# The assumed durations of a list scheduler, set to those of a trace: one core, two layers of a hybrid trunk

## The chip, the cores and the metric

The kernel runs on one core of a Trainium2 chip (trn2). The metric is the device time of one execution in microseconds (us). A core has engines that run beside each other, each in the order in which its own instructions were written: TensorE (PE, with its weight loads as PEld), VectorE (DVE), ScalarE (ACT), GpSimd (POOL), and SyncE (SP), which issues DMAs here. An instruction that needs a result of another engine waits on a semaphore, and everything behind it on its own engine waits with it.

## The reference

Two layers, each `x <- x + W_out(mixer(RMSNorm(x)) * silu(gate))`, on 2048 rows of width 1024 in float32. Layer 0 is stick-breaking attention with 16 heads of 64:

```python
z = jnp.einsum('bthd,bshd->bhts', q[:, t0:kl], k[:, :kl]).astype(jnp.float32) * scale
mask = s_idx < t_idx
log_fail = jnp.where(mask, jax.nn.log_sigmoid(-z), 0.0)
later = lax.cumsum(log_fail, axis=3, reverse=True) - log_fail
a = jnp.where(mask, jnp.exp(jax.nn.log_sigmoid(z) + later), 0.0)
outs.append(jnp.einsum('bhts,bshd->bthd', a.astype(v.dtype), v[:, :kl]))
```

Layer 1 is multi-head latent attention (MLA) with 8 heads: queries and keys come from low-rank latents, are normed per head, a part of 64 is rotated, and a causal softmax follows. Both project into and out of width 1024 with products that the kernel splits into a high and a low part for precision.

## The kernel before

No order of instructions is written by hand. The program first records all work as operations (`Op`: an engine, an assumed duration in ns, the calls, what it depends on, a priority), and then `Sched.issue` plays them through once: for each engine it keeps the time at which the engine would be free, takes from those that are ready the operation that could start first (all that could start within 60 ns of the engine's being free count as equal, and then the lower priority number, that is the earlier work, goes first), issues it, and adds its duration. A result is taken to be usable on another engine a fixed `LAT` after that (120 ns for PE and ACT, 180 for DVE, 150 for POOL). Tiles in SBUF and PSUM come from rings of a few buffers, and a ring with no free buffer holds an operation back as well. What comes out is one order for each engine; the chip then runs it, with real waits. The durations stand in the helpers of the class `Chip`: `mm` (products on PE), `turn` (transpositions on PE), `tt` and `split_sb` (element-wise products and differences), `ts` (a tile times a scalar), `select` (the causal mask on POOL), `fill` (memset).

The work around the change:

- Layer 0 (lines of `proj0` and `attn0`) goes over 8 pairs of heads (`hp`) and 4 groups (`j`) of 512 rows. `proj0` makes q, k, v and gate of a stage with products `pj<-xn,w`, 24 of 512 columns for each of the four. `attn0` takes the 512 rows in four parts (`rt`) against the groups `g` of keys up to `j`. One unit is: two products `z<-ks,qd` into a PSUM bank (ring of 3), two sigmoids on ACT (`a<-z`, `z<-z`), a running product on DVE (`pp<-z,...`, a scan), the product `a<-a,pp` on POOL (and the mask `select` where `g` is `j`), four transpositions `t<-ident,a` on PE, a split of their result on ACT and DVE (`at<-t`), and, when four units are done, products `av<-at,vv`. The projection of the next stage is recorded behind each stage and given priorities spread over it, so that its products fill PE between the units.
- Then come the output projection of layer 0, the latents and gates of layer 1, and MLA (`proj1`, `attn1`): 8 heads by 4 groups, five products for a `z`, a maximum on DVE (`nm`), an exponential on ACT (`s<-z,nm`), a scaling on POOL (`s<-s,c,ri`), transpositions `t<-ident,s`, a split (`pt`), products `av<-pt,vv`. The output projection of layer 1 ends the program.

Of the kernel before, what the change touches and what calls it, by code (L numbers as in the profile page):

```python
# [11 lines left out]
F32 = mybir.dt.float32  # L12
# [3 lines left out]
ALU = mybir.AluOpType  # L16
# [261 lines left out]
def R(x):  # L278
    if isinstance(x, Buf):
        return x.tile  # L280
    return x.resolve() if isinstance(x, Ref) else x


def refs(*xs):
    return [x.all() if isinstance(x, Buf) else x for x in xs if isinstance(x, (Buf, Ref))]


class Chip:
# [4 lines left out]
        self.eng = {"dve": nc.vector, "pool": nc.gpsimd}  # L293

    def mm(self, out, l, r, start, stop, n=G):
        self.s.add("pe", max(n / 2.4, 107.0) + 3.0,
                   lambda: self.nc.tensor.matmul(R(out), lhsT=R(l), rhs=R(r), start=start, stop=stop),  # L297
                   refs(out), refs(l, r))

    def turn(self, out, src, ident):  # L300
        self.s.add("pe", 109.0, lambda: self.nc.tensor.transpose(R(out), R(src), R(ident)), refs(out), refs(src, ident))  # L301

    def act(self, out, src, func, n=G, bias=None, scale=None, accum=None):
        def call():
# [10 lines left out]
        self.s.add("act", 60.0 + 0.833 * n + 93.0 * extra, call, refs(out, accum), refs(src, bias, scale))  # L315

    def tt(self, eng, out, a, b, op, n=G):
        ns = 70.0 + 1.045 * n if eng == "dve" else 155.0 + 2.1 * n
        self.s.add(eng, ns, lambda: self.eng[eng].tensor_tensor(out=R(out), in0=R(a), in1=R(b), op=op),  # L319
                   refs(out), refs(a, b))  # L320

# [3 lines left out]
                   refs(out), refs(a, b))  # L325

    def ts(self, eng, out, a, s1, s2, op0=ALU.mult, op1=ALU.mult, n=G):
        ns = 60.0 + 0.6 * n if eng == "dve" else 90.0 + 1.3 * n
        self.s.add(eng, ns, lambda: self.eng[eng].tensor_scalar(out=R(out), in0=R(a), scalar1=R(s1), scalar2=R(s2),  # L329
                                                                op0=op0, op1=op1),  # L330
                   refs(out), refs(a, s1, s2))
# [33 lines left out]

    def select(self, x, base, fill):

        self.s.add("pool", 300.0,
                   lambda: self.nc.gpsimd.affine_select(out=R(x), in_=R(x), compare_op=ALU.is_ge, fill=fill, base=base,
                                                        pattern=[[-1, P]], channel_multiplier=1),  # L370
                   refs(x), refs(x))

    def fill(self, out, v):
        self.s.add("pool", 40.0, lambda: self.nc.gpsimd.memset(R(out), v), refs(out), [])

    def dma(self, out, src, kb):
        self.s.add("sp", kb * 1024 / 360.0 + 100.0, lambda: self.nc.sync.dma_start(out=R(out), in_=R(src)),
# [7 lines left out]
def trunk(ctx: ExitStack, tc: tile.TileContext, x, w0, wo0, g0, g1, wlat, wgate, gqa, gkva,  # L385
# [7 lines left out]
    C = Chip(nc, sched)  # L393
# [27 lines left out]
    ident = const.tile([P, P], F32, "ident")  # L421
    sched.add("pool", 1000.0, lambda: make_identity(nc, R(ident)), refs(ident), [])
    def causal(dst, base, fill):

        mtmp = pa.tile([P, G], F32, "tmp", 2)[:, 0:P]
        C.fill(mtmp, 0.0)
        C.select(mtmp, base, fill)
        C.copy("dve", dst, mtmp, P)
# [14 lines left out]

    def split_sb(hi, lo, src, n, eng="pool"):
        C.act(hi, src, AF.Copy, n)
        C.tt(eng, lo, src, hi.bitcast(F32), ALU.subtract, n)

    def rstd(pl, ss, n, dim, name, bufs=2):
        v = pl.tile([P, n], F32, name + "v", 2)
# [54 lines left out]
    def load_w(hp, u, early=None):  # L504
        w = pw.tile([P, 2, KD, P], F32R, "w", 4)
        for n, raw in enumerate(early or ()):
            k = slice(4 * n, 4 * n + 4)
            split_sb(w[:, 0, k], w[:, 1, k], raw, 4 * P, "dve" if n else "pool")
        if early:
            ws[hp, u] = w  # L510
            return
        for k in range(0, KD, 2):
            raw = pw.tile([P, 2, P], F32, "wraw", 4)
            C.dma(raw, w0[hp, u, :, k:k + 2, :], 128)
            split_sb(w[:, 0, k:k + 2], w[:, 1, k:k + 2], raw, 2 * P)
        ws[hp, u] = w
# [77 lines left out]
    def attn0(hp, j):  # L594
# [47 lines left out]
        yh = pa.tile([P, 2, G], F32R, "yh")  # L642
        C.tt("dve", y, y, gt, ALU.mult)
        split_sb(yh[:, 0, :], yh[:, 1, :], y, G)
        C.dma(y_d[j, :, hp], yh.all().bitcast(F32), 512)

# [514 lines left out]
```

## Time and profile before

| what | value |
|---|---|
| median of 3 runs | 3061.82 us (3061.26 to 3068.74) |
| the profiled execution | 3061.58 us, its span 3059.9 us |
| busy PE | 2978.5 us, 97% of the span, 15728 matmuls |
| busy DVE, ACT, POOL | 66%, 61%, 49% |
| mean granted TensorE clock | 0.996 |

The span runs from the first to the last instruction; 1.7 us of the execution lie around it. The profile's page gives each engine's busy time, then the span in 40 slices, the DMA queues, the chain of work that ended last, and groups of instructions with the idle time before them. A matmul's record is longer than the time after which the next one starts, since they are pipelined, so that a busy PE can still lose a little.

### The profile page before, as it was taken

How to read it: one execution, taken by the hardware profiler on the slowest of the kernel's cores; microseconds unless marked ns; L12 is line 12 of the kernel's file. 1: busy time of each engine (PE TensorE's matmuls, PEld its weight loads, DVE VectorE, ACT ScalarE, POOL GpSimd, SP SyncE). 2: the span in 40 equal slices, each digit the busy share in tenths (PEclk: the TensorE clock that was granted, in tenths of full speed). 3: DMA queues.
4: the chain of work that ended last, by engine and by line, in shares of the span. 5: the costliest groups of instructions: out<-in, count | busy, mean ns of one | idle time of the engine just before them, and what ended most of it. 6: DMA issues, size and time to landing. Idle time of an engine off the chain costs nothing.

```text
span 3059.9 us, 48542 instructions
## 1 busy us (share of the span) xinstructions
PE 2978.5 (97%) x15728; PEld 2486.1 (81%) x15728; DVE 2024.9 (66%) x3553; ACT 1865.3 (61%) x4635; POOL 1491.4 (49%) x2931
## 2 busy tenths in 40 slices
PE   8899999999999999999999999999999999999999
PEld 6678888888888888888778888878888888888787
DVE  5777896978868778787863231047778777778511
ACT  5676786867768677786852132247777776777400
POOL 4664664756647565574652120136456455555200
PEclk9899999999999999999999999999999999999999
DMA  6253334344243342433339673142222232223462
GB/s 241 104 172 124 130 105 140 109 138 148 81 152 103 125 152 83 150 112 115 126 122 324 243 274 117 69 158 83 78 92 72 86 104 66 75 78 93 160 219 103
DMA packets 134797, 399.87 MB, mean 131 GB/s; under 512 B 16656, under 2 KB 39696, under 8 KB 131984
## 3 DMA queue, kind: packets, MB, share of 16 engines
q1 hardware_dynamic: 134544, 396.76, 38.3%
q8 instruction: 126, 2.06, 0.3%
q14 instruction: 127, 1.04, 0.1%
HBM read 272.97 MB, written 98.57 MB: 121 GB/s over the span
## 4 chain that ended last, share of the span: by engine, by line
PE 75%; DVE 11%; ACT 7%; issue 3%; POOL 2%; DMA 2%; POOLq 0%; DVEq 0%; ACTq 0%; SPq 0%
PE pj L297 30%; PE z L297 21%; PE av L297 12%; PE t L301 9%; DVE pp L342 3%; PE t L297 3%; DVE at L319 1%; DVE pt L319 1%; PE pj L301 1%; ACT s L312 1%; ACT a L312 1%; DVE qs L329 1%; DVE y L319 1%; DVE nm L349 1%; ACT j L312 1%
## 5 line engine op out<-in xcount | busy, mean ns | idle before, releaser
L297 PE MATMUL pj<-xn,w 128*128 128x512 f32 x3072 | 863.6, 402 | 2.0 <-DVE qd L319 1.9
L319 POOL TENSOR_TENSOR a<-a,pp 128x512 f32<-128x512 f32 (+3 forms) x640 | 611.6, 958 | 474.0 <-DVE pp L342 437.4
L297 PEld LDWEIGHTS pj<-xn,w 128*128 128x128 f32 x3072 | 545.4, 188 | 100.0 <-issue 3.7
L342 DVE TENSOR_TENSOR_SCAN pp<-z,cy,a 128x512 f32<-128x512 f32 x384 | 484.1, 1273 | 43.8 <-ACT z L312 39.8
L312 ACT ACTIVATE at<-t 128x512 fp32r<-128x512 f32 (+3 forms) x640 | 340.8, 535 | 156.7 <-PE t L301 154.6
L319 DVE TENSOR_TENSOR at<-t,at 128x512 fp32r<-128x512 f32 (+3 forms) x640 | 377.8, 599 | 84.4 <-ACT at L312 79.5
L312 ACT ACTIVATE a<-z 128x512 f32<-128x512 f32 (+3 forms) x640 | 335.5, 535 | 115.7 <-PE z L297 93.0
L297 PE MATMUL z<-ks,qd 128*128 128x512 f32 (+3 forms) x1280 | 365.2, 377 | 13.7 <-DVE pp L342 9.0
L297 PE MATMUL av<-at,vv 128*128 128x512 f32 (+3 forms) x1280 | 376.1, 379 | 2.1 <-DVE at L319 2.1
L301 PE MATMUL t<-ident,a 128*128 128x128 f32 x2176 | 343.6, 274 | 8.9 <-POOL a L319 4.3
L301 PEld LDWEIGHTS t<-ident,a 128*128 128x128 f32 x2176 | 271.6, 141 | 83.3 <-POOL a L319 7.9
L312 ACT ACTIVATE z<-z 128x512 f32<-128x512 f32 (+3 forms) x640 | 338.7, 536 | 0.7
L329 POOL TENSOR_SCALAR s<-s,c,ri 128x512 f32<-128x512 f32 (+3 forms) x280 | 200.9, 729 | 172.9 <-DVE ri L360 128.1
L297 PEld LDWEIGHTS z<-ks,qd 128*128 128x128 f32 x1280 | 225.2, 190 | 66.6 <-DVE pp L342 20.9
L297 PE MATMUL av<-pt,vv 128*128 128x512 f32 (+2 forms) x960 | 266.3, 384 | 5.0 <-DVE pt L319 3.9
L297 PE MATMUL z<-knt,qn 128*128 128x512 f32 (+2 forms) x960 | 256.8, 376 | 12.1 <-ACT s L312 11.8
L312 ACT ACTIVATE s<-z,nm 128x512 f32<-128x512 f32 (+2 forms) x320 | 199.8, 627 | 102.7 <-DVE nm L349 68.0
L297 PEld LDWEIGHTS av<-at,vv 128*128 128x128 f32 x1280 | 223.1, 190 | 38.0 <-DVE at L319 5.5
L319 DVE TENSOR_TENSOR pt<-t,pt 128x512 fp32r<-128x512 f32 (+1 forms) x312 | 184.3, 606 | 98.6 <-ACT pt L312 96.5
L342 DVE TENSOR_TENSOR_SCAN pp<-z,later 128x128 f32<-128x128 f32 (+3 forms) x256 | 204.3, 814 | 46.8 <-ACT z L312 28.5
L312 ACT ACTIVATE pt<-t 128x512 fp32r<-128x512 f32 (+1 forms) x312 | 163.3, 536 | 72.6 <-PE t L301 70.3
L297 PEld LDWEIGHTS z<-knt,qn 128*128 128x128 f32 x960 | 160.4, 189 | 35.8 <-ACT s L312 17.9
(234 smaller groups left out, 4945.5 us busy)
## 6 DMA issues: line engine op xcount, KB each, us to landing
xn<-xn_d SPq DMA_DIRECT2D x224, 512.0 KB, 4.7
xn_d<-xn SPq DMA_DIRECT2D x64, 512.0 KB, 3.8
y_d<-yh SPq DMA_DIRECT2D x64, 512.0 KB, 2.6
y<-y_d SPq DMA_DIRECT2D x60, 512.0 KB, 5.1
qd<-qd SPq DMA_DIRECT2D x64, 256.0 KB, 3.1
xk<-xn_d SPq DMA_DIRECT2D x32, 512.0 KB, 6.1
cqt<-c_d SPq DMA_DIRECT2D x16, 1024.0 KB, 5.0
ckv<-c_d SPq DMA_DIRECT2D x32, 512.0 KB, 3.7
```

What stands on the lines that cost most here:

```text
L297: lambda: self.nc.tensor.matmul(R(out), lhsT=R(l), rhs=R(r), start=start, stop=stop),
L301: self.s.add("pe", 109.0, lambda: self.nc.tensor.transpose(R(out), R(src), R(ident)), refs(out), refs(src, ident))
L312: self.nc.scalar.activation(R(out), R(src), func, **kw)
L319: self.s.add(eng, ns, lambda: self.eng[eng].tensor_tensor(out=R(out), in0=R(a), in1=R(b), op=op), refs(out), refs(a, b))
L329: self.s.add(eng, ns, lambda: self.eng[eng].tensor_scalar(out=R(out), in0=R(a), scalar1=R(s1), scalar2=R(s2), op0=op0, op1=op1), refs(out) ...
L342: lambda: self.nc.vector.tensor_tensor_scan(R(out), R(a), R(b), initial=R(init), op0=ALU.mult, op1=op),
L349: lambda: self.nc.vector.tensor_reduce(out=R(out), in_=R(src), axis=AX.X, op=op, **kw),
```

## The change

Only numbers that `Sched.issue` adds up are changed; every operation, tile, dependence and priority stays. So the same instructions come out in another order on each engine, and the DMAs with them.

```diff
     def mm(self, out, l, r, start, stop, n=G):
-        self.s.add("pe", max(n / 2.4, 107.0) + 3.0,
+        self.s.add("pe", max(n * 0.446, 0.33 * n + 34.0, 110.0),
...
     def turn(self, out, src, ident):
-        self.s.add("pe", 109.0, lambda: self.nc.tensor.transpose(R(out), R(src), R(ident)), refs(out), refs(src, ident))
+        self.s.add("pe", 110.0, lambda: self.nc.tensor.transpose(R(out), R(src), R(ident)), refs(out), refs(src, ident))
...
     def tt(self, eng, out, a, b, op, n=G):
-        ns = 70.0 + 1.045 * n if eng == "dve" else 155.0 + 2.1 * n
+        ns = 70.0 + 1.045 * n if eng == "dve" else 124.0 + 1.785 * n
...
     def ts(self, eng, out, a, s1, s2, op0=ALU.mult, op1=ALU.mult, n=G):
-        ns = 60.0 + 0.6 * n if eng == "dve" else 90.0 + 1.3 * n
+        ns = 120.0 + 0.6 * n if eng == "dve" else 90.0 + 1.3 * n
...
     def select(self, x, base, fill):
-        self.s.add("pool", 300.0,
+        self.s.add("pool", 240.0,
...
     def fill(self, out, v):
-        self.s.add("pool", 40.0, lambda: self.nc.gpsimd.memset(R(out), v), refs(out), [])
+        self.s.add("pool", 70.0, lambda: self.nc.gpsimd.memset(R(out), v), refs(out), [])
...
     def split_sb(hi, lo, src, n, eng="pool"):
         C.act(hi, src, AF.Copy, n)
-        C.tt(eng, lo, src, hi.bitcast(F32), ALU.subtract, n)
+        C.tt(eng, lo, src, hi.bitcast(F32), ALU.subtract, n + (56 * n) // 256 if eng == "pool" else n)
```

At the sizes that occur most, in ns: a product of 512 columns on PE 216 before, 228 now; `a<-a,pp` of 512 columns on POOL 1230 before, 1038 now; a mask 300, now 240; `kn` (128 columns) on DVE 137, now 197; a memset 40, now 70. The split differences on POOL stay nearly where they were (1230, now 1238, at 512 columns).

Three places on PE show what the orders become. The first is in the first head pair, while stages are still short. In the order before, the products `z<-ks,qd` of the second group of rows stand close together, the one of 256 columns in the second row:

```order
L297 MATMUL pj<-xn,w 128x512 x3
L297 MATMUL z<-ks,qd 128x256 x2
L297 MATMUL pj<-xn,w 128x512 x3
L297 MATMUL z<-ks,qd 128x384 x2
L297 MATMUL pj<-xn,w 128x512 x3
L297 MATMUL z<-ks,qd 128x512 x4
L301 MATMUL t<-ident,a 128x128 x2
L297 MATMUL z<-ks,qd 128x512 x2
L301 MATMUL t<-ident,a 128x128 x3
L297 MATMUL z<-ks,qd 128x512 x4
L297 MATMUL z<-ks,qd 128x128 x2
L301 MATMUL t<-ident,a 128x128 x4
```

Now the same products stand earlier, among those of the projection:

```order
L297 MATMUL pj<-xn,w 128x512 x30
L297 MATMUL z<-ks,qd 128x512 x2
L297 MATMUL pj<-xn,w 128x512 x3
L297 MATMUL z<-ks,qd 128x128 x2
L297 MATMUL pj<-xn,w 128x512 x3
L297 MATMUL z<-ks,qd 128x256 x2
L297 MATMUL pj<-xn,w 128x512 x6
L301 MATMUL pj<-ident,tmp 128x128 x4
L297 MATMUL pj<-xn,w 128x512 x3
L297 MATMUL z<-ks,qd 128x384 x2
L297 MATMUL pj<-xn,w 128x512 x3
L301 MATMUL t<-ident,a 128x128 x4
```

The transpositions that belong to the `z` of 256 columns (`t<-ident,a` x2) stand five rows behind it before; now they come eleven rows behind the last one shown, with fifteen more products of the projection, two of another `z` and six `av` between.

The second place is in the steady part of layer 0, near 493 us, and comes again at the same point of each head pair but the first, seven times. Before, a unit's `z` of 512 columns stands just ahead of the first row here, and its transpositions are the last row:

```order
L297 MATMUL pj<-xn,w 128x512 x9
L301 MATMUL t<-ident,a 128x128 x3
L297 MATMUL pj<-xn,w 128x512 x3
L297 MATMUL z<-ks,qd 128x512 x2
L297 MATMUL pj<-xn,w 128x512 x3
L301 MATMUL t<-ident,a 128x128 x4
L297 MATMUL pj<-xn,w 128x512 x3
L301 MATMUL t<-ident,a 128x128 x4
L297 MATMUL pj<-xn,w 128x512 x3
L297 MATMUL z<-ks,qd 128x512 x2
L297 MATMUL av<-at,vv 128x512 x2
L301 MATMUL t<-ident,a 128x128 x4
```

Now the same unit's `z` is the first row, and its transpositions are the last:

```order
L297 MATMUL z<-ks,qd 128x512 x2
L297 MATMUL pj<-xn,w 128x512 x3
L301 MATMUL t<-ident,a 128x128 x4
L297 MATMUL pj<-xn,w 128x512 x3
L297 MATMUL z<-ks,qd 128x512 x2
L301 MATMUL t<-ident,a 128x128 x4
L297 MATMUL pj<-xn,w 128x512 x3
L297 MATMUL av<-at,vv 128x512 x2
L301 MATMUL t<-ident,a 128x128 x4
```

Between them stood 27 products of 512 columns and 11 transpositions, and now stand 13 and 8.

The third place is where MLA begins. Before, the last `z` of a stage (first two rows) is followed by two more `z` and fifteen products of the projection before its tiles `s` are transposed:

```order
L297 MATMUL z<-knt,qn 128x512 x3
L297 MATMUL z<-kpt,qpt 128x512 x2
L297 MATMUL pj<-wukv,ckv 128x256 x9
L297 MATMUL z<-knt,qn 128x512 x3
L297 MATMUL z<-kpt,qpt 128x512 x2
L297 MATMUL z<-knt,qn 128x512 x3
L297 MATMUL z<-kpt,qpt 128x512 x2
L297 MATMUL pj<-wuq,cqt 128x384 x6
L301 MATMUL t<-ident,s 128x128 x8
```

Now eight transpositions of the next projection are all that stands between:

```order
L297 MATMUL z<-knt,qn 128x512 x3
L297 MATMUL z<-kpt,qpt 128x512 x2
L301 MATMUL pj<-ident,kn 128x128 x4
L301 MATMUL pj<-ident,kq 128x128 x4
L301 MATMUL t<-ident,s 128x128 x8
```

## Rows read from the trace of the kernel before

**Rows 1.** The page: the span, and PE's busy time, share and instructions.

```profile
span 3059.9 us, 48542 instructions
PE 2978.5 (97%) x15728; PEld 2486.1 (81%) x15728; DVE 2024.9 (66%) x3553; ACT 1865.3 (61%) x4635; POOL 1491.4 (49%) x2931
```

**Rows 2.** Stretches: length, busy time (instructions) by engine, clock, DMA share, GB/s.

```profile
78.00:106.00 28.00, 22.39 (x101) 16.61 (x100) 21.39 (x31) 20.98 (x46) 21.29 (x42) 0.76 0.27 108
138.00:153.00 15.00, 11.59 (x50) 8.07 (x48) 11.73 (x16) 11.43 (x24) 14.31 (x22) 0.77 0.09 37
230.00:1454.00 1224.00, 1219.81 (x6490) 1014.04 (x6489) 980.75 (x1281) 902.26 (x1922) 740.36 (x1684) 1.00 0.37 123
1500.00:1530.00 30.00, 25.66 (x135) 19.26 (x134) 27.97 (x35) 25.60 (x55) 22.49 (x47) 1.00 0.47 172
2070.00:2907.00 837.00, 809.64 (x4706) 695.44 (x4705) 629.43 (x1663) 582.12 (x1813) 422.73 (x616) 1.00 0.28 90
2907.00:2984.00 77.00, 77.00 (x335) 62.68 (x335) 7.74 (x12) 0.00 (x0) 0.00 (x0) 1.00 0.62 217
```

**Rows 3.** Groups by line and shape: busy us, mean ns, idle before, releasers.

```profile
L319 POOL TENSOR_TENSOR a<-a,pp 128x512 f32<-128x512 f32 x448 | 490.3, 1095 | 285.6 <-DVE pp L342 259.4 <-ACT at L312 8.9 <-ACT z L312 4.1
L342 DVE TENSOR_TENSOR_SCAN pp<-z,cy,a 128x512 f32<-128x512 f32 x384 | 484.1, 1273 | 43.8 <-ACT z L312 39.8 <-POOL a L319 1.8 <-POOL cy L364 0.5
L312 ACT ACTIVATE z<-z 128x512 f32<-128x512 f32 x448 | 265.5, 601 | 0.7
L312 ACT ACTIVATE a<-z 128x512 f32<-128x512 f32 x448 | 263.3, 599 | 67.3 <-PE z L297 50.2 <-POOL cy L364 5.7 <-POOL a L369 4.5
L329 POOL TENSOR_SCALAR s<-s,c,ri 128x512 f32<-128x512 f32 x211 | 163.5, 785 | 172.9 <-DVE ri L360 128.1 <-PE z L297 14.2 <-ACT pt L312 9.5
L349 DVE TENSOR_REDUCE nm<-z 128x1 f32<-128x512 f32 x192 | 130.5, 684 | 23.7 <-PE z L297 22.6
L369 POOL TENSOR_SCALAR_AFFINE_SELECT a<-a 128x128 f32<-128x128 f32 x256 | 74.1, 292 | 3.0
L329 DVE TENSOR_SCALAR kn<-kn,akr 128x128 f32<-128x128 f32 x128 | 46.0, 416 | 6.6 <-POOL akr L324 6.5
```

**Rows 4.** PE's waits, 230 to 1454 us: us in total, times, longest.

```profile
PE z L297 <- DVE pp L342: 2.4, 7, 0.4
PE t L301 <- DVE at L319: 1.2, 6, 0.2
```

**Rows 5.** PE's waits, 2070 to 2907 us, the longest two in total.

```profile
PE z L297 <- ACT s L312: 10.9, 17, 1.4
PE av L297 <- DVE pt L319: 3.9, 11, 0.6
```

**Rows 6.** PE in order of time, 78 to 97 us: start, us, instruction, [idle before].

```profile
81.35 0.33 PE L301 MATMUL t<-ident,a 128*128 128x128 f32 x1 [0.68 <-POOL a L319]
82.85 0.33 PE L301 MATMUL t<-ident,a 128*128 128x128 f32 x1 [1.17 <-POOL a L369]
...
86.40 1.11 PE L301 MATMUL t<-ident,a 128*128 128x128 f32 x3 [2.35 <-POOL a L319]
```

**Rows 7.** DVE in order of time, 62 to 96 us.

```profile
69.08 1.41 DVE L319 TENSOR_TENSOR ks<-pj,ks 64x512 fp32r<-64x512 f32 x2 [6.46 <-ACT ks L312]
...
74.05 0.69 DVE L319 TENSOR_TENSOR vv<-pj,vv 128x512 fp32r<-128x512 f32 x1 [2.04 <-ACT vv L312]
...
76.90 0.69 DVE L319 TENSOR_TENSOR y<-av,y 64x512 f32<-64x512 f32 x1 [2.17 <-ACT y L312]
```

**Rows 8.** PE in order of time, 489.7 to 502 us: the second place.

```profile
493.13 0.62 PE L297 MATMUL z<-ks,qd 128*128 128x512 f32 x2
...
498.03 0.60 PE L301 MATMUL t<-ident,a 128*128 128x128 f32 x4
498.39 0.94 PE L297 MATMUL pj<-xn,w 128*128 128x512 f32 x3
499.17 0.60 PE L301 MATMUL t<-ident,a 128*128 128x128 f32 x4
...
501.23 0.60 PE L301 MATMUL t<-ident,a 128*128 128x128 f32 x4
```

## The prediction, made before the changed kernel ran

> **What bounds the kernel now.** I read the page first: PE is busy for 2978.5 us of a span of 3059.9 us, so only 81.4 us of it are idle, and the next engine, DVE, is at 66% [rows 1]. The question of any other order is therefore not how much work there is (it is the same) but how often PE stands still. So I read the stretches next [rows 2]. In the steady part of layer 0, from 230 to 1454 us, PE idles for 1224.00 - 1219.81 = 4.2 us: nothing is to be had there, and something can be lost. Idle time lies at the edges and in MLA: 28.00 - 22.39 = 5.6 us from 78 to 106 us and 3.4 us from 138 to 153 us, both in the first head pair and both at a mean granted clock of 0.76 to 0.77, that is with part of the stretch at 1.2 GHz instead of 2.4; 4.3 us from 1500 to 1530 us, where no projection is left to fill in; and 27.4 us in the 837 us of MLA. A stretch in which PE waits for nothing prices a product of 512 columns: 77.00 us for 335, that is 0.23 us each [rows 2]. Transpositions I price at 0.11 us: from one row of four to the next such row pass 499.17 - 498.03 = 1.14 us, of which three products take 0.69 [rows 8].
>
> **The new numbers against the trace.** The PE price goes from 0.216 to 0.228 us, and the trace says 0.23; there the change is right. The GpSimd product goes from 1230 ns to 1038, where the record of one has 1095 ns; the mask from 300 to 240, recorded at 292; the small DVE product from 137 to 197, recorded at 416 [rows 3]. The memset moves by 30 ns, the split differences by 8, and they decide nothing. A record can be longer than the time for which it holds its engine, so these differences alone prove no error. But they all change the same thing: how far behind a unit's `z` its transpositions are put. Before, the scheduler took PE for 5% faster and POOL for 0.14 us slower than their rows, so each transposition stood a few tenths of a us of PE work later than needed. That surplus is taken out.
>
> **Term A, the first head pair.** The waits from 80 to 86 us are PE's for `a`, 0.68, 1.17 and 2.35 us [rows 6]. What was late is the scans ahead of POOL: DVE had stood idle for 6.46, 2.04 and 2.17 us at 69 to 77 us [rows 7], because the `z` that it needs came only afterwards, and then got its scans in a row. In the order before, 6 products of the projection, 4 of `z` at full width and one pair of 384 columns (some 0.17 us each) stand between the `z` of 256 columns and its transpositions: 10 x 0.23 + 2 x 0.17 = 2.6 us. In the new order 31 products of 512 columns, 9 transpositions and three narrower pairs stand there: 31 x 0.23 + 9 x 0.11 + 0.9 = 9.0 us, so the scans fall into DVE's idle time. The stretch is worth at most its idle 5.6 us and what the lower clock cost, 0.24 x 28 = 6.7 us, together 12 us. But the last four scans and POOL's norm products still come together behind it, and in the next stage (138 to 153 us) the `z` of 256, 384 and 512 columns stand closer to their transpositions than before. I take half, -6 us, and keep -12 and +3 (the second cluster doubled, the first unchanged) for the range.
>
> **Term B, the steady part of layer 0.** At the second place PE had 27 x 0.23 + 11 x 0.11 = 7.4 us between a unit's `z` and its transpositions (the trace has 501.23 - 493.59 = 7.6, the `z` pair taking 0.46 of what follows 493.13 [rows 8]); now it has 13 x 0.23 + 8 x 0.11 = 3.9 us. The chain between, by its own rows, is 0.60 + 0.60 on ACT, 1.27 on DVE and 1.10 on POOL, 3.57 us [rows 3], after the 0.16 us by which the pair of `z` (recorded at 0.62) outlasts its two slots of 0.23 [rows 8]: 3.73 us and the four hand-overs. So the unit stands at its limit, with no surplus for a queue on ACT, DVE or POOL. Counted in this way along both orders over the 361 units of 512 columns that start between 230 and 1454 us (narrower products between in proportion, none under 0.11), the median distance goes from 6.6 to 5.5 us, and the units with less than 4.5 us from 12 to 72. A unit that is too close costs what the present waits cost: 1.2 us in 6, 0.2 each, to 2.4 us in 7, 0.34 each [rows 4]. If none of the 60 new ones waits, the term is 0; if all do at 0.34, 20 us. Since the orders of DVE, ACT and POOL move with PE's, I let half of them wait at 0.2: +6 us.
>
> A rule speaks for the upper end. "TensorE: Matmul & The Clock Gate" of the Trainium skill (section Back-to-back issue gap) gives an isolated product N/2.4 + 2.5 ns, an estimate of 216 ns for 512 columns, which is the old table's number. By it the unit at the second place would have 3.7 us, under its chain, all 60 would wait, and the sum below would be 14 us larger. The trace differs: 0.23 us in a stretch without a wait [rows 2]. So I follow the row.
>
> **Term C, the start of MLA.** At the third place the eight transpositions leave 0.9 us between the last `z` and the transpositions of `s`. The maximum and the scaling alone take 0.68 + 0.79 = 1.5 us [rows 3], with an exponential between that is not under them; PE must wait there, some 0.6 to 2 us, once or twice. Before, 25 products stood between. +2 us, 0 to +4.
>
> **Term D, the rest of MLA.** PE's largest wait there is for a `z` bank that ACT has not read out yet, 10.9 us in 17 waits, then 3.9 us in 11 waits for `pt` [rows 5]. The new order pulls the projection's pieces apart at some of these places and packs them at others; the count of close units rises by about a sixth. The larger price of the small DVE products ought to help, since eight of them stand ahead of the maxima in each projection. From -11 (all bank waits gone) to +11 (as many again); I take -2.
>
> **Term E, 1500 to 1530 us.** With no filler left the order hardly matters; one unit stands 0.9 us closer. +1, from 0 to +3. DMA issues move on SP too, but what PE waits for is DVE, ACT and POOL in the rows above; the first transfer after each `z` operand has several us of stage ahead of it, and I put it at 0.
>
> **The sum.** -6 + 6 + 2 - 2 + 1 = +1 us on the profiled execution of 3061.6 us (span 3059.9 and 1.7 around it, 0.2 below the median of the runs): 3062.6, given as 3063 us, no change that can be told. A difference of 0.3%, 9.2 us, is about what a measurement of this kernel tells from none.
>
> **Rivals.**
> - *Slower, by the lost surplus.* One mechanism: in the steady part of layer 0 transpositions (and `av` behind them) wait for `a`. If all 60 wait at 0.34 us, B is 20 and the time 3061.6 - 6 + 20 + 2 - 2 + 1 = 3077 us; it decides, alone, from B = 14.2 on, where the sum is over 9.2 us, that is from 42 of them. For it: the unit at the second place is at its chain's limit, and seven head pairs repeat it. Against it: POOL is at 49%, DVE at 66% [rows 1], and a wait of PE makes the next unit's distance longer.
> - *Faster, at the edges.* The stall of the first head pair goes with its low clock (A = -12) and all bank waits of MLA go (D = -11): 3061.6 - 12 + 6 + 2 - 11 + 1 = 3048 us. For it: PE's idle time before 160 us follows directly from DVE's idle time ahead of it [rows 6, 7]. Against it: a new cluster may bring the low clock back.
> - *The order changes and nothing else.* PE is the bound at 97% [rows 1], and any reasonable order reaches it: B, C and D at 0, A at -6, some 3056 us, also within 0.3%.
>
> **Chances.** No change (the forecast and the third rival) 0.42, slower 0.30, faster 0.28. All terms at their low ends make 3039, at their high ends 3103. The range cuts about 1 in 10 on each side: 3042 to 3092 us.
>
> **What will show it.** A: idle time and clock of PE from 78 to 106 us; right if DVE no longer idles 6 us ahead of it and the clock there stays at 2.4 GHz for most of the stretch. B: PE's idle time from 230 to 1454 us (4.2 us before) and a group of waits `t` <- POOL `a` that is absent now; 10 us expected, over 18 the first rival is right. C: a wait of `t` for `s` near 2070 us. D: `z` <- ACT `s` in MLA at 9 us. The prediction is wrong if PE's idle time in MLA moves by more than 10 us, or if a stretch at 1.2 GHz comes up where there was none.

## The result, and the profile after

| | before | after |
|---|---|---|
| median of 4 runs | 3061.68 us (3061.26 to 3068.74) | 3115.93 us (3114.93 to 3117.41) |
| ratio, 95% interval | | 1.0172, 1.0154 to 1.019 |
| span of the profiled execution | 3059.9 us | 3115.6 us |

The kernel became 54 us slower; forecast was no change. 3116 us lies above the range (3042 to 3092) and above the sum with all terms at their high ends (3103). The page of after, which answers to [rows 1]:

```profile
span 3115.6 us, 48356 instructions
PE 3011.4 (97%) x15728; PEld 2482.2 (80%) x15728; DVE 2025.1 (65%) x3553; ACT 1877.4 (60%) x4635; POOL 1501.1 (48%) x2931
```

The same 15728 matmuls, and yet PE is *busy* for 32.9 us more; its idle time grew by only 104.2 - 81.4 = 22.8 us. The stretches of after ([rows 2] has those of before; the end of MLA lies 56 us later now, so the last two windows are moved by as much):

```profile
78.00:106.00 28.00, 22.72 (x108) 18.02 (x107) 22.33 (x31) 20.60 (x44) 21.15 (x39) 0.76 0.24 95
138.00:153.00 15.00, 9.71 (x37) 6.00 (x36) 11.88 (x14) 10.61 (x22) 14.46 (x25) 0.78 0.09 37
230.00:1454.00 1224.00, 1216.40 (x6397) 989.62 (x6396) 962.08 (x1263) 894.86 (x1897) 736.92 (x1666) 1.00 0.37 122
2126.00:2963.00 837.00, 802.53 (x4622) 683.60 (x4621) 622.53 (x1626) 576.38 (x1774) 416.15 (x604) 1.00 0.28 88
2963.00:3040.00 77.00, 77.00 (x335) 62.67 (x334) 7.73 (x12) 0.00 (x0) 0.00 (x0) 1.00 0.62 216
```

In 1224 us of layer 0 PE now gets through 6397 matmuls, 93 fewer than before, although it idles for only 7.6 us there (4.2 before). So idle time is not the measure. Two views show where the rest is. First, PE in order of time near the second place:

```profile
504.26 0.62 PE L297 MATMUL z<-ks,qd 128*128 128x512 f32 x2
504.96 0.66 PE L301 MATMUL t<-ident,a 128*128 128x128 f32 x4
505.37 0.96 PE L297 MATMUL pj<-xn,w 128*128 128x512 f32 x3
```

and the weight loads (PEld) of the same moment:

```profile
504.03 0.42 PEld L297 LDWEIGHTS z<-ks,qd 128*128 128x128 f32 x2
504.96 0.42 PEld L301 LDWEIGHTS t<-ident,a 128*128 128x128 f32 x4 [0.51 <-POOL a L319]
```

The two `z` products need 0.46 us, so the transpositions could start at 504.72; they start at 504.96. These 0.24 us are lost, and the PE rows print no idle time: the record of the last `z` lasts until 504.88 (a record of 512 columns is some 0.39 us long, the time until the next start, its slot, 0.23), and the 0.08 us left are too short to be printed. The weight load, which comes first and carries the wait, shows it. So here are PEld's waits from 230 to 1454 us. Before:

```profile
PEld z L297 <- DVE pp L342: 9.3, 18, 0.8
PEld pj L297 <- issue: 2.6, 7, 0.4
PEld t L301 <- POOL cy L364: 1.9, 6, 0.3
```

After:

```profile
PEld t L301 <- POOL a L319: 27.0, 103, 0.6
PEld z L297 <- DVE pp L342: 18.1, 33, 1.1
PEld t L301 <- issue: 3.6, 11, 0.4
PEld t L301 <- POOL a L369: 3.2, 13, 0.4
```

The group that was absent, `t` <- POOL `a`, is now the largest: 103 waits. The products of `z` wait twice as long for a PSUM bank that a scan (`pp`) still reads. Part of a PEld wait passes under the running product, so these totals are not a loss. For the loss I use start times alone: from each matmul's start to the next one's, less its price in the new table (0.228 us at 512 columns, 0.110 at 128). What is left over I call the **excess**; summed over stretches of equal PE work it can be compared between orders. In us:

| stretch (us of PE work) | before | after | difference | term |
|---|---|---|---|---|
| first head pair (0 to 120) | 35.9 | 38.9 | +3.0 | A: -6 |
| rest of layer 0 (120 to 1440) | 28.4 | 49.4 | +21.0 | B: +6 |
| output projection, latents, gates (1440 to 1920) | 25.3 | 33.1 | +7.8 | E: +1 |
| start of MLA (1920 to 2040) | 19.6 | 33.9 | +14.3 | C: +2 |
| rest of MLA (2040 to 2760) | 49.6 | 59.2 | +9.6 | D: -2 |
| all, with the last projection (1.1 each) | 159.9 | 215.6 | +55.7 | +1 |

The sum is the difference of the spans. Each column comes from one execution. How well a row repeats can be read from kernels (described below) whose TensorE order is the same over that row: with the VectorE price alone, and with the new TensorE price in MLA only, the rest of layer 0 has the order of before and 28.8 and 28.4; with the new TensorE price ahead of MLA only, the order of MLA is that of before, with 18.1 at its start and 48.8 in the rest. So a row repeats to some 2 us.

The start times also say ahead of which product the time is lost. In the rest of layer 0, 12.2 of the 21.0 us lie ahead of `z` (10.6 before, 22.8 after) and 8.3 ahead of `t` (5.2 and 13.5). In MLA nearly all of it lies ahead of the products and transpositions of the projection (`pj`): 13.4 of the 14.3 at its start (8.0 and 21.4) and 8.5 of the 9.6 in the rest (13.1 and 21.6).

### The profile page after: what moved, and what is told of

Its sections match the earlier page's. It is cut to its first block, busy times and chain, and to the rows that moved or that the text cites. A ratio compares the mean times of both kernels' runs of the same rounds, so it can differ in the third digit from the quotient of the medians.

```text
span 3115.6 us, 48356 instructions
## 1 busy us (share of the span) xinstructions
PE 3011.4 (97%) x15728; PEld 2482.2 (80%) x15728; DVE 2025.1 (65%) x3553; ACT 1877.4 (60%) x4635; POOL 1501.1 (48%) x2931
## 4 chain that ended last, share of the span: by engine, by line
PE 76%; DVE 8%; ACT 6%; POOL 5%; issue 3%; DMA 1%; POOLq 0%; ACTq 0%; DVEq 0%; SPq 0%
PE pj L297 30%; PE z L297 21%; PE av L297 12%; PE t L301 10%; PE t L297 2%; DVE pp L342 2%; POOL a L319 1%; PE pj L301 1%; ACT s L312 1%; POOL s L329 1%; DVE nm L349 1%; ACT z L312 1%; DVE pt L319 1%; DVE kn L329 1%; ACT j L312 1%
## 5 line engine op out<-in xcount | busy, mean ns | idle before, releaser
L297 PE MATMUL z<-ks,qd 128*128 128x512 f32 (+3 forms) x1280 | 376.5, 382 | 17.9 <-DVE pp L342 15.6
L301 PE MATMUL t<-ident,a 128*128 128x128 f32 x2176 | 349.2, 276 | 9.6 <-POOL a L319 5.4
L301 PEld LDWEIGHTS t<-ident,a 128*128 128x128 f32 x2176 | 264.0, 141 | 104.3 <-POOL a L319 37.9
L297 PE MATMUL z<-knt,qn 128*128 128x512 f32 (+2 forms) x960 | 257.4, 376 | 10.1 <-ACT s L312 10.0
```

Source lines behind the costliest of these rows:

```text
L301: self.s.add("pe", 110.0, lambda: self.nc.tensor.transpose(R(out), R(src), R(ident)), refs(out), refs(src, ident))
```

## The experiments

**The theory.** In the sums of the scheduler the old prices left every hand-over between PE and the other engines some tenths of a us more than it needed, above all because PE was taken for 5% too fast; small queues on ACT, DVE and POOL disappear in that surplus. Calibrated prices take it out. **Rivals:** any change of the numbers scatters the order, and the time with it; or one price, at one place, does it all.

**One part of the change alone.** Each kernel is before with one helper of after: `mm` and `turn`; `tt`, `select`, `fill` and `split_sb`; `ts`.

```diff
-        self.s.add("pe", max(n / 2.4, 107.0) + 3.0,
+        self.s.add("pe", max(n * 0.446, 0.33 * n + 34.0, 110.0),
...
-        self.s.add("pe", 109.0, lambda: self.nc.tensor.transpose(R(out), R(src), R(ident)), refs(out), refs(src, ident))
+        self.s.add("pe", 110.0, lambda: self.nc.tensor.transpose(R(out), R(src), R(ident)), refs(out), refs(src, ident))
```

> The change's TensorE price alone (512 columns 0.228 us in place of 0.216), all other prices as before. Theory of the lost surplus: the scheduler took PE for some 5% too fast, so a chain of 3.6 us was covered by 5% more work than it needed; this part alone should cost 15 to 35 of the 54 us, 3077 to 3097 us, with a group of PEld waits t <- POOL a from 230 to 1454 us between that of before (under 1 us) and that of after (27.0 us in 103). Rival, that any new order scatters: anywhere from 3045 to 3100 us, and the parts do not add up to the whole. Rival, that one price alone does it: 3062 or 3116 us.

```diff
-        ns = 70.0 + 1.045 * n if eng == "dve" else 155.0 + 2.1 * n
+        ns = 70.0 + 1.045 * n if eng == "dve" else 124.0 + 1.785 * n
...
-        self.s.add("pool", 300.0,
+        self.s.add("pool", 240.0,
...
```

> The change's GpSimd prices alone (product of 512 columns 1038 ns in place of 1230, mask 240 in place of 300, and the two small ones), all other prices as before. Theory of the lost surplus: a and the masked tiles are held for ready 0.06 to 0.19 us earlier than before, less than a slot of PE, so 10 to 30 of the 54 us, 3072 to 3092 us, and again the waits t <- POOL a. Rival, that any new order scatters: anywhere from 3045 to 3100 us. Rival, that one price alone does it: 3062 or 3116 us.

```diff
-        ns = 60.0 + 0.6 * n if eng == "dve" else 90.0 + 1.3 * n
+        ns = 120.0 + 0.6 * n if eng == "dve" else 90.0 + 1.3 * n
```

> The change's price of the small VectorE product alone (137 to 197 ns at 128 columns), all other prices as before. Theory of the lost surplus: this price goes up, so it adds distance rather than taking it: 3053 to 3065 us, and no waits t <- POOL a. Rival, that any new order scatters: 3045 to 3100 us.

Measured: TensorE price alone 3115.77 us (1.0174, 1.0159 to 1.019); GpSimd prices 3067.34 us (1.0016, 1.0007 to 1.0026); VectorE price 3054.93 us (0.9974, 0.9963 to 0.9984). The TensorE price alone costs as much as the whole change, more than I had expected of it, and the GpSimd prices, which I had thought of as up to half of it, cost little. In the rest of MLA they even gain (excess 43.3, for 49.6), although they take surplus out: there the theory has the wrong sign. The VectorE price leaves layer 0 as it was (excess 28.8, for 28.4) and gains in the rest of MLA, 39.5 for 49.6: of PE's 17 waits of `z` for ACT `s` [rows 5] one of 0.2 us is left there. PE's waits from 2070 to 2900 us in that kernel, the longest two in total:

```profile
PE pj L297 <- DVE qpt L319: 3.4, 4, 0.9
PE t L301 <- DVE s L329: 2.6, 1, 2.6
```

With the TensorE price alone PEld's waits from 230 to 1454 us are of a different mix:

```profile
PEld t L301 <- POOL a L319: 13.3, 53, 0.4
PEld z L297 <- DVE pp L342: 9.9, 27, 0.8
PEld av L297 <- DVE at L319: 7.9, 13, 0.9
```

The excess of the rest of layer 0 is 47.4, nearly that of after, with half the waits for `a`. With the GpSimd prices alone there are nearly as many (15.8 us in 42), and the excess is only 30.4. So the loss isn't the distance from `z` to `t` alone: `av` behind the split, and `z` behind its bank, lose as well. Against before, the TensorE price alone loses 5.7 us ahead of `z`, 6.7 ahead of `t` and 5.9 ahead of `av`.

**The surplus, given back and taken away by another number.** `LAT` is the hand-over that the scheduler assumes; a price is not touched.

```diff
-    LAT = {"pe": 120.0, "act": 120.0, "dve": 180.0, "pool": 150.0, "sp": 2000.0}
+    LAT = {"pe": 220.0, "act": 220.0, "dve": 280.0, "pool": 250.0, "sp": 2000.0}
```

in after:

> The kernel after, with 100 ns more of hand-over assumed behind every PE, ACT, DVE and POOL instruction. Theory of the lost surplus: a unit's chain from z over ACT, ACT, DVE and POOL to the transposition has five hand-overs, so it gets 0.5 us of distance back, about what the old prices gave: 3055 to 3080 us, and the PEld waits t <- POOL a (27.0 us in 103) fall under 8 us. Rival, that any new order scatters: no tie to the distance, 3060 to 3130 us. If it stays at 3105 to 3125 us, distance is not what was lost.

in before, with 100 ns less (20, 20, 80, 50):

> The kernel before with all its old prices, and 100 ns less of hand-over assumed behind each PE, ACT, DVE and POOL instruction. It takes the distance away by another way than the TensorE price. Theory of the lost surplus: 5 hand-overs of 100 ns are 0.5 us of a unit's distance, so it becomes like after, 3085 to 3130 us, and from 230 to 1454 us the start of PE's work falls back by 10 to 25 us. Rival, the PE price alone is what hurts, by the ratio of the engines: 3050 to 3075 us.

in before, with 100 ns more:

> The kernel before with 100 ns more of hand-over assumed behind every PE, ACT, DVE and POOL instruction. Theory of the lost surplus: layer 0's steady part loses less still (some 5 us), MLA too; but the start of MLA cost 15 us when the TensorE price was lowered, and may again: 3045 to 3075 us. Rival, that before stands at an optimum of distance and every step away costs: 3075 to 3095 us.

Measured: after with 100 ns more 3063.62 us (1.0004, 0.9994 to 1.0013), no longer to be told from before, and the PEld group `t` <- `a` down from 27.0 us to 5.9 in 25 waits; before with 100 ns less 3138.44 us (1.0244, 1.0229 to 1.0259), worse than expected; before with 100 ns more 3062.03 us (0.9998, 0.9988 to 1.0008). In the rest of layer 0 the excess goes 66.5, 28.4, 15.5 from 100 ns less to 100 ns more in before, and from 49.4 to 32.6 in after. Both parts of it answer: ahead of `z` the loss is 18.2, 10.6 and 2.1 us in before, ahead of `t` 27.4, 5.2 and 2.5; in after, `z` goes from 22.8 to 15.7 and `t` from 13.5 to 3.5. The rest of MLA goes the same way (56.8, 49.6, 42.8 in before; 59.2 to 43.4 in after). Another 9.1 us of what after gets back lie at the start of MLA, where the same 100 ns cost before 18.2, so for that part the surplus is not shown to be the cause. From 230 to 1454 us in before, first with 100 ns less:

```profile
230.00:1454.00 1224.00, 1206.88 (x6319) 976.99 (x6318) 963.18 (x1253) 883.41 (x1884) 744.66 (x1659) 1.00 0.36 119
```

and with 100 ns more:

```profile
230.00:1454.00 1224.00, 1224.00 (x6552) 1023.24 (x6551) 988.80 (x1292) 912.20 (x1937) 749.23 (x1701) 1.00 0.38 125
```

6319, 6490 [rows 2] and 6552 matmuls in the same 1224 us: what was at 4.2 us of idle time had 13 us of excess to give, which the idle time could not show. That before with 100 ns more is no faster in all comes from the start of MLA, which lost 37.8 in place of 19.6.

**The size of the TensorE price.** Half of the step, and a step of the same size in the other direction:

```diff
-        self.s.add("pe", max(n / 2.4, 107.0) + 3.0,
+        self.s.add("pe", 0.5 * (max(n / 2.4, 107.0) + 3.0) + 0.5 * max(n * 0.446, 0.33 * n + 34.0, 110.0),
```

> The kernel before with the TensorE price half way between old and new (222 ns at 512 columns). Theory of the lost surplus: part of the loss, between that of before and that of after, 3070 to 3105 us. Rival, that any new order scatters: 3045 to 3075 us or 3115 and more, without regard to the price. Rival, a threshold (one place that tips over): 3062 or 3116 us.

```diff
-        self.s.add("pe", max(n / 2.4, 107.0) + 3.0,
+        self.s.add("pe", 2.0 * (max(n / 2.4, 107.0) + 3.0) - max(n * 0.446, 0.33 * n + 34.0, 110.0),
```

> The kernel before with the TensorE price moved by the same 12 ns in the other direction (204 ns at 512 columns), further from the trace. Theory of the lost surplus: there is more distance still, and few waits of this kind are left to remove in layer 0; MLA may gain: 3040 to 3065 us, not slower. Rival, that the old price was right for some other reason (an optimum): 3075 to 3115 us, slower on this side too.

Measured: 3073.62 us (1.0029, 1.0017 to 1.0041) and 3074.22 us (1.0033, 1.0021 to 1.0045). The second is slower, against the theory as I had put it. By stretch it falls into two parts: at 204, 216, 222 and 228 ns for 512 columns the rest of layer 0 has an excess of 23.4, 28.4, 30.5 and 47.4, in the order of the surplus; the start of MLA has 34.9, 19.6, 24.6 and 35.5, in no order. The first head pair and the stretch of the output projection, latents and gates lose at 204 too (40.2 for 35.9 and 30.3 for 25.3).

**Where it acts.** The new TensorE price for what is recorded ahead of MLA only (a flag in `mm`, switched where MLA's pools are opened), and the converse:

```diff
+        self.pe_new = True
...
-        self.s.add("pe", max(n / 2.4, 107.0) + 3.0,
+        self.s.add("pe", max(n * 0.446, 0.33 * n + 34.0, 110.0) if self.pe_new else max(n / 2.4, 107.0) + 3.0,
...
+    C.pe_new = False
     ISQ = 1.0 / math.sqrt(QK1)
```

> The new TensorE price for what is recorded before layer 1's MLA (layer 0, its output projection, the latents and gates), the old one for MLA and the last projection; all other prices old. Theory of the lost surplus: it acts where the price acts: about 25 us of the 54 up to 2040 us, then the start and the rest of MLA as in before, 3080 to 3095 us. Rival, one place decides (the start of MLA): 3062 to 3070 or 3105 to 3116 us.

> The converse of the kernel with the new TensorE price ahead of MLA: the old price up to the gates of layer 1, the new one for MLA and the last projection. Theory of the lost surplus, acting where the price acts: layer 0 as before, the start of MLA and the rest of it as with the new price, so 3062 + 54 - 22 = 3094 us, 3080 to 3100. Rival, that what is lost in MLA comes from the order that layer 0 leaves behind: 3060 to 3070 us.

Measured: 3085.08 us (1.0066, 1.005 to 1.0083) and 3095.63 us (1.0111, 1.0096 to 1.0126). Against the runs of before beside them that is +21.6 and +31.5, together 53.1; the price in the whole program cost 53.5. It acts in both layers, and no one place does it. That the sum is so close is partly luck, for the stretches don't add up: the rest of layer 0 lost 13.0 here (41.4) and 19.0 in the whole program (47.4), the rest of MLA 17.1 (66.7) and 8.9 (58.5). These two kernels keep `turn` at its old 109 ns, where the kernel with the TensorE price alone has 110, so they are not exact halves of it. In layer 0 this 1 ns is the only price in which the first of them differs, and it moves the excess by 6.0 us: so much an order does scatter, and the rival is right to that extent. The steps from 23.4 to 30.5 between the lower TensorE prices are no larger than that; those of 100 ns of hand-over are (38.1, 12.9 and 16.8).

**The two small parts together**, after with the old `mm`:

> The kernel after with the old TensorE price: the GpSimd and VectorE prices new. Theory of the lost surplus, with the TensorE price as its main part: the two small effects seen alone add, 3062 + 5 - 7 = 3060 us, 3053 to 3067. Rival, that any new order scatters: no such sum, 3045 to 3100 us.

Measured 3067.53 us (1.001, 1.0001 to 1.002). Not the sum: the VectorE price's gain doesn't show on top of the GpSimd prices, which alone already had the rest of MLA at 43.3 (43.4 here).

**The start of MLA.** If surplus is what layer 0 lacks, and the VectorE price helps MLA, the two should come together. 100 ns more of hand-over for all that is recorded ahead of MLA, and the new price in `ts`:

```diff
+        self.cover = 100.0
...
-            op.lat = self.LAT[eng]
+            op.lat = self.LAT[eng] + (self.cover if eng != "sp" else 0.0)
...
-        ns = 60.0 + 0.6 * n if eng == "dve" else 90.0 + 1.3 * n
+        ns = 120.0 + 0.6 * n if eng == "dve" else 90.0 + 1.3 * n
...
+    sched.cover = 0.0
     ISQ = 1.0 / math.sqrt(QK1)
```

> The old TensorE and GpSimd prices, 100 ns more of hand-over for all that is recorded ahead of MLA, none more in MLA, and the new price of the small VectorE product. Theory of the lost surplus: with the added hand-over in the whole program layer 0's steady part lost 13 us less than before, what follows it 3 more, and the start of MLA gave 18 back; with the new VectorE price MLA lost 10 us less. Here the first and the last come together without the start of MLA: 3063 - 13 + 3 - 10 = 3043 us, 3036 to 3052, faster than both. Rival, the start of MLA gives it back whatever the prices are there: 3055 to 3068 us.

Measured 3056.22 us (0.9973, 0.9962 to 0.9985): the rival. The rest of layer 0 and the rest of MLA came out as forecast (15.6 and 39.4), but the start of MLA lost 36.8. So two more: the same with the added hand-over ended earlier, ahead of the latents, and after with the old TensorE price from there to the eighth stage of MLA.

```diff
+    sched.cover = 0.0
     for k in range(KD):
         xkload(0, k)
```

> As the kernel with 100 ns more of hand-over ahead of MLA and the new VectorE price, but the added hand-over ends with the output projection of layer 0: latents, gates and MLA are planned without it. TensorE's order from the first product of MLA on is then, over its first 1384 operations, that of the kernel with the VectorE price alone, whose start of MLA lost 19 us in place of 37. Theory, the start of MLA depends on its order alone: 3056 - 17 = 3039 us, 3034 to 3047, and PE's excess there 18 to 21 us. Rival, what layer 0 saves is given back there by something else (a DMA or a buffer that is late at that time): 3052 to 3060 us.

```diff
+    C.pe_new = False
     for k in range(KD):
         xkload(0, k)
...
     for n, (h, j) in enumerate(stages):
+        C.pe_new = n >= 8
```

> The kernel after with the old TensorE price for what is recorded from the latents to the eighth stage of MLA, the new one elsewhere. TensorE's order at the start of MLA is then near that of the kernel with the GpSimd and VectorE prices alone, which lost 23 us there in place of 34. Theory: layer 0 loses its 20 us as in after, the start of MLA gets 10 to 14 back, 3098 to 3110 us. Rival, the start of MLA follows what comes before it: 3112 to 3118 us.

Measured: 3040.54 us (0.993, 0.9916 to 0.9943), the fastest of all, faster than before and after; and 3091.06 us (1.0094, 1.008 to 1.0108). In the first the start of MLA lost 17.3, a little under the 18 to 21 expected, and the rest of layer 0 15.7. Against before its excess is 21 us smaller: 12.7 in the rest of layer 0, 9.2 in the rest of MLA, and small amounts both ways elsewhere. PE from 2010 to 2135 us, first with the added hand-over up to MLA:

```profile
2010.00:2135.00 125.00, 106.94 (x560) 91.91 (x559) 81.09 (x212) 78.26 (x274) 60.06 (x93) 0.90 0.30 93
```

then with its earlier end:

```profile
2010.00:2135.00 125.00, 113.18 (x665) 98.13 (x663) 93.11 (x256) 91.19 (x318) 72.26 (x112) 1.00 0.34 103
```

105 matmuls more in the same 125 us, and no stretch at the lower clock; at 0.90 the clock alone is worth up to 0.10 x 125 = 12.5 us of the 19.5 by which the starts of MLA differ (an estimate). The rest of layer 0 loses as much in both, so what is lost here is not a delay that layer 0 leaves; it goes with the order from the latents on, and from the first product of MLA on TensorE's order is the one which lost 19.2 with the VectorE price alone. After with the old price at that place gained more than expected, 25 us: 10 at the start of MLA (23.7), 8 in the latents and gates, 7 in the rest of MLA, while the rest of layer 0 stayed at 48.8. What makes an order of this stretch good or bad, beyond the waits below, I did not isolate.

## Why the prediction was wrong

**B failed, and took the forecast with it.** The mechanism, lost surplus, is shown for the rest of layer 0: there a higher assumed hand-over undoes much of the loss, a lower one makes more of it, by 13 to 38 us, and the highest TensorE price costs the most. The step that failed is "If none of the 60 new ones waits, the term is 0; if all do at 0.34, 20 us", halved to +6: it counted one hand-over, from a unit's `z` to its `t`, and had no term for the others. The stretch lost +21.0, past the end that I had set. The waits that I counted cost 8.3 us ahead of `t`, not far from the +6; 12.2 us are lost ahead of `z`, which waits for a bank that a scan still reads. In detail:
- The count of close units is not the quantity. With the TensorE price alone no unit of the 361 stands under 4.5 us (12 before, 72 after, counted alike), and the excess is 47.4 against 49.4. The time from `a` being ready to its transposition did shrink: in before a unit in 20 has less than 0.38 us, half less than 0.88; in after a quarter have less than 0.10, half less than 0.27. It does not give the size of the loss either: with the GpSimd prices alone half have less than 0.52, with the TensorE price alone half less than 0.63, and the excess is 30.4 and 47.4.
- The surplus on POOL was read from records. In before the median time from the start of one `a<-a,pp` of 512 columns to POOL's next start is 1.04 us, that behind a mask 0.24, and that behind `kn` on DVE 0.20. So the new prices are right there, and the old one was 0.19 us too long for `a`, where I had 0.14.
- The price of a wait, and the sign "over 18 the first rival is right", came from PE's idle rows [rows 4]. After, PE idles for 7.6 us in that stretch, under the 10 that I had expected with no change, while its excess grew by 21. What the prediction said of it first, that nothing is to be had there and something can be lost, was half wrong for the same reason: 13 us were to be had.

**A**, the gain of 6 us, did not come: +3.0. DVE still idles ahead of the first cluster, and the clock in it is 0.76 again. DVE in order of time after, for [rows 7]:

```profile
68.88 1.41 DVE L319 TENSOR_TENSOR ks<-pj,ks 64x512 fp32r<-64x512 f32 x2 [6.19 <-ACT ks L312]
```

PE in order of time, for [rows 6]:

```profile
84.06 0.63 PE L301 MATMUL t<-ident,a 128*128 128x128 f32 x4 [1.58 <-DVE at L319]
86.36 0.80 PE L297 MATMUL av<-at,vv 128*128 128x512 f32 x1 [1.68 <-ACT at L312]
```

The longer distance to the transpositions only moved the wait: `t` and `av` now wait behind the split (`at`) where they waited for `a`. That the second cluster keeps the low clock was in the range (+3).

**C** was sized from one wait, and the stretch has many. PE's waits after, from 2050 to 2204 us, which is the start of MLA there (the four longest in total):

```profile
PE pj L301 <- DVE qn L319: 2.9, 1, 2.9
PE pj L301 <- DVE sm L336: 2.7, 1, 2.7
PE z L297 <- DMA qpt<-qpt: 2.2, 1, 2.2
PE pj L301 <- DVE vv L319: 2.0, 1, 2.0
```

Before, the same work, from 2018 to 2158 us:

```profile
PE pj L297 <- ACT qs L312: 3.1, 4, 1.1
PE z L297 <- ACT s L312: 2.6, 4, 0.9
PE pj L297 <- DVE vv L319: 2.0, 1, 2.0
PE z L297 <- DMA cqt<-c_d: 1.4, 1, 1.4
```

The wait of `t` for `s` that I named is hardly there: two of PEld's, 0.6 us in all. The transpositions of the next projection (`pj`, L301) stand too early and hold PE for 2 to 3 us each, for their own operands or their bank. The projection that fills in elsewhere is itself what PE waits for here. +14.3 where I had at most 4. That lost surplus causes it is not shown.

**D** had a wrong sign: +9.6 for -2. `z` <- ACT `s` stayed (9.8 us in 15 waits, for 10.9 in 17 [rows 5]). The small VectorE price does what I had hoped of it, -10.1 by itself, but the TensorE price costs +8.9 by itself, and with all prices new the gain is gone. The loss lies ahead of the projection's products, not at the bank waits from which I had sized the term.

**E** lies in a row of the table that is wider than its term: output projection, latents and gates lost 7.8. The end of layer 0 with the first output products (1440 to 1560 us of work) lost 1.5, near the +1; the latents and gates (1680 to 1920) lost 5.3, and for them the sum had no term.

The rival *slower* had the right direction. That its B (20) is near the 21.0 is luck: it put all of it down to transpositions that wait for `a`, and 8.3 us lie there. Its 3077 us took over A, C and D, which were wrong by 9 + 12 + 12 us, and left out the latents. *Faster, at the edges* named, in its D, the gain that the VectorE price gives alone.

The step from the skill deserves a second look. In after 335 products of 512 columns again take 77.00 us, 0.23 each, so the row that I followed holds. The Trainium skill's "TensorE: Matmul & The Clock Gate" (section Back-to-back issue gap) has an estimate of 216 ns for an isolated product, which these runs don't agree with. Yet the table with that number gives the faster kernel; in layer 0, as the runs with other hand-overs show, its error stood in for a margin.

## What to carry to other kernels

A list scheduler needs a margin on its hand-overs beside its prices; where wrong prices have been giving the margin, calibrating them alone takes it away. Put the margin where the bound engine has filler, and not in a stretch where it waits for each step of a chain: here 100 ns on `LAT` up to the end of layer 0's output projection, with the VectorE price, made 3040.54 us, for 3062 and 3116. That kernel has the old TensorE and GpSimd prices; the new ones with a margin in those stretches alone were not run, and with 100 ns everywhere they come to 3063.62, where before is. What makes one order of the start of MLA lose 17 us and another 37 stays open. And when an engine looks 97% busy, don't ask its idle time what can be gained or lost; count what it gets through in a fixed stretch, and read the waits of its weight loads.

## What the runs showed of the hardware

- Waits of PE up to 0.16 us (a record of 0.39 us less its slot of 0.23, at 512 columns) leave no idle time in its rows, and of longer ones only the rest shows: in 1224 us PE was busy for 1216.40 us with 6397 matmuls, for 1219.81 with 6490 [rows 2], for 1224.00 with 6552. The weight loads show the wait.
- Idle time at the start of MLA was followed by a lower clock. After, PE stands idle for 2.02 us ahead of 2078.97, 1.20 ahead of 2081.42 and 2.15 ahead of 2091.79 us, and the granted clock is at 1.2 GHz for 3.4 us from 2081.9 and again from 2092.1. The window around them (the clock is the third number from the end):

```profile
2078.00:2098.00 20.00, 15.68 (x77) 0.83 0.29 74
```

Over the whole start of MLA PE spends 13.7 us at 1.2 GHz after and 3.4 before; half of the difference, 5 us of the 14.3 there, is the most that the clock itself can have cost (an estimate). In the output projection, latents and gates it is 13.7 us for none; half of that lies in one window of the latents after:

```profile
1815.00:1835.00 20.00, 17.50 (x68) 0.83 0.67 228
```

Such a stretch where there was none is a sign of being wrong that the prediction had named. In all, PE spends 52.8 us at the lower clock after and 28.7 before; at half the speed these 24 us more are worth at most 12 of the 54 (an estimate).
